# Jensen-Shannon divergence on one core: the bias of the logarithms as an immediate in place of a per-partition pointer

## The chip, the core and the metric

The kernel runs on one core of a Trainium2 chip. A core has several engines that run side by side, each with its own instruction queue: TensorE (PE, matmuls into PSUM), VectorE (DVE, elementwise work and reductions), ScalarE (ACT, functions from tables such as the logarithm), GpSimd (POOL) and SyncE (SP). SP, ACT and POOL can also start DMA transfers between the main memory (HBM) and the on-chip memory (SBUF). The metric is the time of one execution on the device in microseconds (us), the median of several; lower is better.

## What is computed

```python
def reference(p, q):                      # both 1024 x 4096, fp32, rows sum to 1
    m = 0.5 * (p + q)
    kl_pm = np.sum(p * np.log(p / (m + 1e-8) + 1e-8), axis=-1)
    kl_qm = np.sum(q * np.log(q / (m + 1e-8) + 1e-8), axis=-1)
    return (0.5 * (kl_pm + kl_qm)).astype(np.float32)      # 1024 values
```

The kernel takes the quotients apart: it forms ln(S·p), ln(S·q) and ln(S·(p+q)/2 + S·1e-8), with S = 6634 (`SHIFT`), stores the logarithms as 16-bit floats, and sums p·ln p + q·ln q − (p+q)·ln m over each row, times one half. The constant that is added inside a logarithm is the instruction's bias, the factor is its scale.

## The kernel before

The 1024 rows are cut into 8 row groups of 128 rows, one row to a partition, and each row group has 4096 columns. For every group there is one tile that holds p and q side by side as 16-bit floats. Three lists of widths, `LOADS`, `LOGS` and `SUMS`, cut the columns of every group into pieces: one for the transfers, one for the logarithms of p and q, one for the sum p+q and its logarithm. Pieces of different lists need not coincide. Row group 6, for instance, is loaded in two pieces of 2048 columns (loads 18 and 19), its logarithms are cut at 2304 (q18 and q19), and its sums at 1536 and 2816 (c21, c22, c23).

Loads. The first two pieces are loaded as fp32 by SP (p) and ACT (q), lines 153 and 154. All others are started by POOL (lines 161 and 162), which converts to 16 bits on the way. They are issued in the order of the columns, p and q in turn, and every load has a place of its own in SBUF, so no load waits for a buffer. At most eight of these transfers are under way: POOL waits for the landing of the one eight places before.

The operations, each with a letter and a number:
- F (line 203, PE): p+q of one sum piece, as matmuls with an identity matrix, into one of two PSUM buffers. For the first two pieces DVE adds instead (a, line 191).
- q (line 215, ACT): ln(S·p) and ln(S·q) of one log piece in a single instruction, into one of four buffers (tile `ab_t`). The bias is the tile `tiny_t`.
- c (line 223, ACT): ln of the sum of one sum piece, out of PSUM, into one of four buffers (tile `c_t`). The bias is the tile `epsc_t`.
- x (lines 234 and 238, DVE), row groups 0 to 2: the difference of the logarithms and its product with p and q.
- s (line 258, DVE), row groups 3 to 7: (p+q)·ln m with a running row sum, the sum read out by a small instruction right behind it.
- m (line 245, DVE), row groups 3 to 7: p·ln p and q·ln q. The last one, m24, is done with its row sum at line 251.
- r (line 272, PE): adds the columns of an x or m product into a PSUM accumulator, as matmuls with half the identity, in steps of 256 columns.
- f (lines 282 and 290, DVE): the final row sum of one row group out of the accumulator.

Every engine works through an order that is written out by hand (`ACT_ORDER`, `PE_ORDER`, `DVE_ORDER`, lines 58 to 72) and does not deviate from it. The last lines of ACT's order are `q18 c21 c22 q19 q20 c23 c24 q21 q22 c25 q23 c26 q24`, and of DVE's order `m18 s21 s22 m19 m20 s23 s24 m21 f6 m22 s25 m23 s26 f7 m24`. A c operation needs its F; an F from the fifth on needs its PSUM buffer back from the s (or c) two pieces before; an m needs its q, an s needs its c, f7 needs the matmuls on m23 and s26. At the end SP writes the result out (line 341).

Before all that, lines 147 to 150 write two one-column tiles with the biases on DVE, and line 156 runs one logarithm on a single column, so that ACT's table is loaded while the first data is on its way.

Of the kernel before, what the change touches and what calls it, by code (L numbers as in the profile page):

```python
# [9 lines left out]
SHIFT = 6634.0  # L10
# [65 lines left out]
def kernel(  # L76
# [6 lines left out]
    nc = tc.nc  # L83
    P = nc.NUM_PARTITIONS
    Alu = mybir.AluOpType
    Act = mybir.ActivationFunctionType
# [8 lines left out]
    fp32 = mybir.dt.float32  # L95
# [25 lines left out]
    small = ctx.enter_context(tc.tile_pool(name="small", bufs=1))  # L121
# [16 lines left out]
    def pq(g, c0, w):  # L138
        if g == 0:
            for i in range(HW):  # L140
                if loads[i] == (g, c0, w):
                    return early[i]
            c0 -= split
            assert c0 >= 0
        return data[g][:, :, c0 : c0 + w]

    tiny_t = small.tile([P, 1], fp32, tag="tiny")
    nc.vector.memset(tiny_t, 1e-30)  # L148
    epsc_t = small.tile([P, 1], fp32, tag="epsc")
    nc.vector.memset(epsc_t, SHIFT * 1e-8)  # L150
    for i in range(HW):
        g, c0, w = loads[i]
        nc.sync.dma_start(out=early[i][:, 0, :], in_=pv[g, :, c0 : c0 + w])
        nc.scalar.dma_start(out=early[i][:, 1, :], in_=qv[g, :, c0 : c0 + w])
    warm = small.tile([P, 1], fp32, tag="warm")
    nc.scalar.activation(out=warm, in_=tiny_t, func=Act.Ln, bias=tiny_t, scale=1.0)  # L156
    ident = small.tile([P, P], fp16, tag="ident")
    make_identity(nc, ident)
    for g, c0, w in loads[HW:]:
# [5 lines left out]
        out=half, in0=ident, scalar1=0.5, scalar2=0.0, op0=Alu.mult, op1=Alu.add  # L165
# [13 lines left out]
    ab, c, s, product, acc = {}, {}, {}, {}, {}  # L179
# [32 lines left out]
    def op_q(i):  # L212
        g, c0, w = logs[i]
        ab_t = lnp.tile([P, 2, w], fp16, tag="ab")
        nc.scalar.activation(  # L215
            out=ab_t, in_=pq(g, c0, w), func=Act.Ln, bias=tiny_t, scale=SHIFT
        )
        ab[i] = ab_t

    def op_c(j):  # L220
        w = parts[j][2]
        c_t = mid.tile([P, SW], fp16, tag="c")
        nc.scalar.activation(  # L223
            out=c_t[:, :w], in_=s[j], func=Act.Ln, bias=epsc_t, scale=SHIFT * 0.5
        )
        c[j] = c_t[:, :w]

# [73 lines left out]
    def uses(i):  # L301
# [16 lines left out]
        + [("s", j) for j in range(NS) if parts[j][0] == g and apart(parts[j])],  # L318
    }
    ops = dict(a=op_a, F=op_F, q=op_q, c=op_c, x=op_x, m=op_m, s=op_s, r=op_r, f=op_f)  # L320
    queues = [
        [(w[0], int(w[1:])) for w in text.split()] for text in (PE_ORDER, ACT_ORDER, DVE_ORDER)
# [49 lines left out]
```

## Time and profile before

| what | us |
|---|---|
| median of 9 runs | 103.49 (103.03 to 104.89) |
| the profiled execution, whole | 103.16 |
| its span, first to last instruction | 101.1 |
| ACT busy / DVE busy / PE busy | 92.7 / 82.1 / 64.2 |
| ACT waiting for loads (L215), three times in all | 2.0 |
| DVE waiting for ACT (L234 and L245) | 10.0 |
| last of the loads issued by POOL | 64.01 |
| last ACT logarithm begins | 95.92 |
| last DVE operation begins | 98.69 |

The span is what the profile shows; the whole time of an execution has another 2.06 us around it. A row of the profile gives engine, line, operation, output tile and input tiles, with shapes as partitions x elements. Tile names that are cut short, such as `t` for the data tiles and `st` for the sums in PSUM, are the program's own. A number in brackets behind a timeline row is how long the engine had been idle before it, and on what. DVE's 10.0 us is the sum of the rows of the view of the waits: 4.2 and 2.7 before line 234, 3.1 before line 245.

### The profile page before, as it was taken

The page shows a single profiled execution, that of the slowest core. Times are in us where ns is not written, and L with a number is a line of the kernel's source. Part 1 is how long each engine was busy: PE and PEld are TensorE (multiplying, and loading weights), DVE is VectorE, ACT ScalarE, POOL GpSimd, SP SyncE. Part 2 cuts the span into 40 slices and gives each one's busy share as a digit, 9 for nine tenths or more (in the row PEclk, how much of TensorE's full clock was granted, in tenths as well). Part 3 has the DMA queues.
Part 4 walks back from the last instruction along what each step waited for, and adds up shares of the span by engine and source line. Part 5 has one row for each costly group of instructions (what it writes and reads, how often), then busy time and mean ns, then how long its engine had stood idle before and what let it go on. Part 6 is the DMA issues. An engine that isn't in the chain of part 4 may idle for free.

```text
span 101.1 us, 1137 instructions
## 1 busy us (share of the span) xinstructions
PE 64.2 (64%) x402; PEld 39.6 (39%) x402; DVE 82.1 (81%) x88; ACT 92.7 (92%) x54; POOL 22.0 (22%) x46
## 2 busy tenths in 40 slices
PE   0048965576588674599669699248488197985250
PEld 0003534324255251445564474135173173834230
DVE  2179967688986935999999998399897999998980
ACT  3789999999999599999999999999999999999910
POOL 7955444242322422222222222200000000000000
PEclk9999999999999999759999999999999999999955
DMA  2999999999999999999999999999999940000000
GB/s 59 355 192 204 209 212 212 211 213 210 212 211 215 216 211 216 212 216 209 217 212 216 212 220 209 214 211 212 216 214 214 211 81 6 0 0 0 0 0 2
DMA packets 6485, 17.34 MB, mean 172 GB/s; under 512 B 848, under 2 KB 1872, under 8 KB 6480
## 3 DMA queue, kind: packets, MB, share of 16 engines
q0 software_dynamic: 5760, 16.29, 82.2%
q1 hardware_dynamic: 432, 0.50, 1.7%
q10 hardware_dynamic: 288, 0.49, 1.4%
q8 instruction: 3, 0.05, 0.2%
q14 instruction: 2, 0.02, 0.0%
HBM read 33.55 MB, written 0.00 MB: 332 GB/s over the span
## 4 chain that ended last, share of the span: by engine, by line
DMA 57%; ACT 18%; issue 11%; DVE 5%; POOL 4%; ACTq 1%; POOLq 0%; DVEq 0%
DMA t<-in_q_dram 57%; ACT ab_t L215 10%; ACT c_t L223 9%; DVE c_t L258 3%; POOL t L161 2%; POOL t L162 2%; ACTq L367 1%; DVE ab_t L245 1%; DVE ab_t L251 0%; DVE junk L290 0%; POOL ident masks.py:199 0%; POOL ident masks.py:197 0%; ACTq L215 0%; ACTq L223 0%; POOLq masks.py:199 0%
## 5 line engine op out<-in xcount | busy, mean ns | idle before, releaser
L215 ACT ACTIVATE ab_t<-t,tiny_t 128x2048 f16<-128x2048 f16 (+15 forms) x25 | 61.5, 2478 | 2.0 <-DMA t<-in_q_dram 2.0
L203 PE MATMUL st<-t,ident 128*128 128x512 f16 (+2 forms) x138 | 34.2, 376 | 13.8 <-DMA t<-in_p_dram 6.4
L272 PEld LDWEIGHTS <-half 128*128 128x128 f16 x264 | 26.1, 101 | 28.9 <-issue 23.7
L223 ACT ACTIVATE c_t<-st,epsc_t 128x1280 f16<-128x1280 f32 (+7 forms) x25 | 32.1, 1316 | 0.0
L272 PE MATMUL acc_t<-ab_t,half 128*128 128x256 f16 (+2 forms) x172 | 21.5, 279 | 14.0 <-DVE ab_t L245 13.7
L245 DVE TENSOR_TENSOR ab_t<-t,ab_t 128x2048 f16<-128x2048 f16 (+6 forms) x13 | 23.1, 1788 | 3.2 <-ACT ab_t L215 3.1
L203 PEld LDWEIGHTS <-ident 128*128 128x128 f16 x138 | 13.6, 101 | 28.6 <-issue 16.0
L234 DVE TENSOR_TENSOR ab_t<-ab_t,c_t 128x2048 f16<-128x2048 f16 (+8 forms) x12 | 14.7, 1224 | 6.9 <-ACT c_t L223 4.2
L258 DVE CUSTOM_DVE_ANT_0 c_t<-st,c_t,run 128x1280 f16<-128x1280 f32 (+3 forms) x10 | 16.0, 1602 | 0.7
L161 POOL DMA_DIRECT2D t<-in_p_dram x20 | 10.8, 541 | 22.3 <-DMA t<-in_p_dram 22.1
L272 PE MATMUL acc_t<-t,half 128*128 128x256 f16 (+1 forms) x92 | 11.8, 276 | 5.5 <-DVE t L238 5.5
L162 POOL DMA_DIRECT2D t<-in_q_dram x20 | 10.7, 535 | 19.7 <-DMA t<-in_q_dram 19.7
L238 DVE TENSOR_TENSOR t<-t,ab_t 128x2048 f16<-128x2048 f16 (+6 forms) x10 | 13.4, 1339 | 0.9
L258 DVE CUSTOM_DVE_ANT_0 c_t<-st,c_t 128x1536 f16<-128x1536 f32 (+1 forms) x5 | 8.2, 1645 | 0.0
L191 DVE TENSOR_TENSOR s<-t 128x320 f32<-128x320 f32 (+1 forms) x2 | 1.3, 658 | 3.2 <-DMA t<-in_q_dram 3.2
L156 ACT ACT_TABLE_LOAD x1 | 1.3, 1283 | 1.7 <-PEq L356 1.7
L290 DVE CUSTOM_DVE_ANT_0 junk<-acc_t,ones,run 128x256 f16<-128x256 f32 x5 | 2.4, 480 | 0.3
L238 DVE TENSOR_TENSOR ab_t<-t,ab_t 128x640 f16<-128x640 f32 (+1 forms) x2 | 2.3, 1158 | 0.1
L223 ACT ACTIVATE c_t<-s,epsc_t 128x320 f16<-128x320 f32 (+1 forms) x2 | 1.4, 679 | 0.0
L282 DVE TENSOR_REDUCE res<-acc_t 128x1 f32<-128x256 f32 x3 | 1.3, 418 | 0.0
L258 DVE DVE_READ_ACCUMULATOR2_ANT run<- 128x1 f32 x15 | 1.2, 83 | 0.0
L148 DVE MEMSET tiny_t<- 128x1 f32 x1 | 0.1, 59 | 0.8 <-PEq L356 0.8
(14 smaller groups left out, 2.7 us busy)
## 6 DMA issues: line engine op xcount, KB each, us to landing
t<-in_p_dram POOLq DMA_DIRECT2D x10, 512.0 KB, 19.4
t<-in_q_dram POOLq DMA_DIRECT2D x10, 512.0 KB, 19.4
t<-in_p_dram POOLq DMA_DIRECT2D x3, 320.0 KB, 13.4
t<-in_q_dram POOLq DMA_DIRECT2D x3, 320.0 KB, 13.3
t<-in_p_dram POOLq DMA_DIRECT2D x2, 352.0 KB, 10.8
t<-in_q_dram POOLq DMA_DIRECT2D x2, 352.0 KB, 11.5
t<-in_p_dram POOLq DMA_DIRECT2D x1, 384.0 KB, 12.8
t<-in_q_dram POOLq DMA_DIRECT2D x1, 384.0 KB, 13.3
```

The costliest lines, as they stand in the source:

```text
L156: nc.scalar.activation(out=warm, in_=tiny_t, func=Act.Ln, bias=tiny_t, scale=1.0)
L161: nc.gpsimd.dma_start(out=v[:, 0, :], in_=pv[g, :, c0 : c0 + w])
L162: nc.gpsimd.dma_start(out=v[:, 1, :], in_=qv[g, :, c0 : c0 + w])
L203: nc.tensor.matmul(out=st[:, b : b + m], lhsT=ident, rhs=v[:, t, b : b + m], start=t == 0, stop=t == 1,)
L215: nc.scalar.activation(out=ab_t, in_=pq(g, c0, w), func=Act.Ln, bias=tiny_t, scale=SHIFT)
L223: nc.scalar.activation(out=c_t[:, :w], in_=s[j], func=Act.Ln, bias=epsc_t, scale=SHIFT * 0.5)
L234: nc.vector.tensor_tensor(out=v, in0=v, in1=c[j].unsqueeze(1).to_broadcast([P, 2, w]), op=Alu.subtract)
L238: nc.vector.tensor_tensor(out=into, in0=u, in1=v, op=Alu.mult)
L245: nc.vector.tensor_tensor(out=ab[i], in0=u, in1=ab[i], op=Alu.mult)
L258: nc.vector.tensor_tensor_reduce(out=c[j], in0=s[j], in1=c[j], scale=-0.5, scalar=before, op0=Alu.mult, op1=Alu.add, accum_out=now,)
L272: nc.tensor.matmul(out=acc[g][:, :m], lhsT=half, rhs=v[:, t, b : b + m], start=k == terms_of[g][0] and n == 0, stop=k == terms_of[g][-1] a ...
L290: nc.vector.tensor_tensor_reduce(out=junk, in0=acc[g][:, :AW], in1=ones, scale=1.0, scalar=before, op0=Alu.mult, op1=Alu.add, accum_out=now,)
```

## The change

Both bias tiles and their memsets go. The logarithms at lines 215 and 223 take their bias as a number that stands in the instruction; scale, function, tiles and order stay. The warm-up logarithm takes a tile of its own, written by one memset, with the default bias and scale, in place of `tiny_t`. In the changed program the lines below the edit move up by three.

```diff
-    tiny_t = small.tile([P, 1], fp32, tag="tiny")
-    nc.vector.memset(tiny_t, 1e-30)
-    epsc_t = small.tile([P, 1], fp32, tag="epsc")
-    nc.vector.memset(epsc_t, SHIFT * 1e-8)
     for i in range(HW):
...
     warm = small.tile([P, 1], fp32, tag="warm")
-    nc.scalar.activation(out=warm, in_=tiny_t, func=Act.Ln, bias=tiny_t, scale=1.0)
+    nc.vector.memset(warm, 1.0)
+    nc.scalar.activation(out=warm, in_=warm, func=Act.Ln)
...
         nc.scalar.activation(
-            out=ab_t, in_=pq(g, c0, w), func=Act.Ln, bias=tiny_t, scale=SHIFT
+            out=ab_t, in_=pq(g, c0, w), func=Act.Ln, bias=1e-30, scale=SHIFT
         )
...
         nc.scalar.activation(
-            out=c_t[:, :w], in_=s[j], func=Act.Ln, bias=epsc_t, scale=SHIFT * 0.5
+            out=c_t[:, :w], in_=s[j], func=Act.Ln, bias=SHIFT * 1e-8, scale=SHIFT * 0.5
         )
```

## The prediction

> **What bounds the kernel now.** I read the page first (engine shares, the 40 slices, the costliest groups), then the waits, then ACT's and DVE's timelines, where the answer lies.
>
> From the page: the shares, two slice rows, and the two groups that the change edits.
>
> ```profile
> PE 64.2 (64%) x402; PEld 39.6 (39%) x402; DVE 82.1 (81%) x88; ACT 92.7 (92%) x54; POOL 22.0 (22%) x46
> ...
> ACT  3789999999999599999999999999999999999910
> ...
> DMA  2999999999999999999999999999999940000000
> ...
> L215 ACT ACTIVATE ab_t<-t,tiny_t 128x2048 f16<-128x2048 f16 (+15 forms) x25 | 61.5, 2478 | 2.0 <-DMA t<-in_q_dram 2.0
> ...
> L223 ACT ACTIVATE c_t<-st,epsc_t 128x1280 f16<-128x1280 f32 (+7 forms) x25 | 32.1, 1316 | 0.0
> ```
>
> ACT is at nine tenths in nearly every slice, so it looks like the bound. But the DMA row is as full until about slice 32 (83 us), and the loads write into tiles that nobody reuses, so their landings do not depend on compute. Two things pace the head: ACT, and a load stream that no ACT saving can hasten. ACT's timeline shows which one is last (start, duration, a merged pair counts as x2):
>
> ```profile
> 34.34 4.56 ACT L215 ACTIVATE ab_t<-t,tiny_t 128x5120 f16<-128x5120 f16 x1 [1.03 <-DMA t<-in_q_dram]
> ...
> 67.53 3.73 ACT L215 ACTIVATE ab_t<-t,tiny_t 128x4096 f16<-128x4096 f16 x1
> 71.12 2.57 ACT L223 ACTIVATE c_t<-st,epsc_t 128x1280 f16<-128x1280 f32 x2
> 73.67 4.13 ACT L215 ACTIVATE ab_t<-t,tiny_t 128x4608 f16<-128x4608 f16 x1
> 77.71 2.74 ACT L223 ACTIVATE c_t<-st,epsc_t 128x1536 f16<-128x1536 f32 x2
> ```
>
> The op at 73.67 is q18. Its 2304 columns of row group 6 reach into load 19, whose q half GpSimd issued at 54.18 (third from last on its timeline). Eight DMAs are in flight there and each takes 19.4 us to land (page, part 6), so it landed at about 73.57: q18 started some 0.1 us after its data, and was not more than that behind. The row at 34.34 is an earlier place of the same kind, with the wait visible.
>
> After 83 us no load is open. There the DVE timeline is the one to read (line 245 is an m op, 258 an s op, 290 an f op, 251 the last):
>
> ```profile
> 77.83 2.56 DVE L245 TENSOR_TENSOR ab_t<-t,ab_t 128x4608 f16<-128x4608 f16 x1 [0.44 <-ACT ab_t L215]
> ...
> 89.91 0.08 DVE L258 DVE_READ_ACCUMULATOR2_ANT run<- 128x1 f32 x1
> 90.08 1.23 DVE L245 TENSOR_TENSOR ab_t<-t,ab_t 128x2048 f16<-128x2048 f16 x1
> 91.22 0.48 DVE L290 CUSTOM_DVE_ANT_0 junk<-acc_t,ones,run 128x256 f16<-128x256 f32 x1
> 91.62 0.08 DVE L290 DVE_READ_ACCUMULATOR2_ANT res<- 128x1 f32 x1
> 91.97 1.23 DVE L245 TENSOR_TENSOR ab_t<-t,ab_t 128x2048 f16<-128x2048 f16 x1 [0.26 <-ACT ab_t L215]
> 93.29 1.68 DVE L258 CUSTOM_DVE_ANT_0 c_t<-st,c_t,run 128x1408 f16<-128x1408 f32 x1
> 94.90 0.08 DVE L258 DVE_READ_ACCUMULATOR2_ANT run<- 128x1 f32 x1
> 94.97 1.09 DVE L245 TENSOR_TENSOR ab_t<-t,ab_t 128x1792 f16<-128x1792 f16 x1
> 96.08 1.42 DVE L258 CUSTOM_DVE_ANT_0 c_t<-st,c_t,run 128x1152 f16<-128x1152 f32 x1
> 97.42 0.08 DVE L258 DVE_READ_ACCUMULATOR2_ANT run<- 128x1 f32 x1
> 97.65 0.48 DVE L290 CUSTOM_DVE_ANT_0 junk<-acc_t,ones,run 128x256 f16<-128x256 f32 x1
> 98.28 0.48 DVE L251 CUSTOM_DVE_ANT_0 ab_t<-t,ab_t,run 128x256 f16<-128x256 f16 x1
> ```
>
> DVE is almost without holes too: it idles at 77.4 for q18, then fractions of a tenth each time it meets a fresh ACT result. The end is set by two engines that run level, behind a load stream that sets their start.
>
> **What the Trainium skill says.** "ScalarE: Activation LUTs", section What ACT_TABLE_LOAD costs, prices an ACTIVATE with a `[128,1]` bias pointer at about 280 ns + 0.833 ns per element and one with immediates at 186 ns, 93 ns less; and says that neighbours overlap by about 93 ns. The trace agrees with the first: 2002 ns for the 2048 form (by-form groups; 280 + 1707 = 1987). The second price has no row here. "Perfetto Trace Analysis", section Optimizing Scalar/DVE Operations, gives the engine-busy overhead of ScalarE as about 93 ns on SBUF and 51 ns on PSUM, the rest of a profiled duration lying beside the next instruction. This lets me ask whether the pointer is in the part that blocks the engine. Start to start, the SBUF op of 3072 at 28.03 gives way to the next at 30.77: 2.74 − 2.56 = 0.18. The PSUM op of 1408 at 26.71 gives way at 28.03: 1.32 − 1.17 = 0.15. So 0.18 against 0.093, and 0.15 against 0.051: in both about 0.09 is over, which is the pointer's price. I take it that the pointer costs 93 ns of issue time. "TensorE: Matmul & The Clock Gate", Part 1, says that TensorE falls to half clock after an idle window of about 3.4 us; the page's PEclk row shows a 7 and a 5 once in mid-run, and 5s at the end.
>
> **The change, part by part.**
> *The 52 logarithms lose their pointer.* ACT's order is the same in the built program, and every wait names the same semaphores; each of L215's 25 and L223's 27 ops (a second row of the page has two of these) gets 93 ns shorter. Gross: 52 × 0.093 = 4.8 us. Bounds for one op: not below 0, as nothing is added to it, and not over the 0.15 to 0.18 of the whole fixed part; I take 0.093, and the end hangs little on it, as the tail below shows.
> *Ahead of q18* lie 39 of the 52, worth 3.6 us. All of it becomes waiting: q18 needs load 19 at 73.57 and started at 73.67, 0.1 later; the row at 34.34 shows ACT after a wait of this kind starting just behind its landing, too. Gain at q18's start: 0 (up to 0.1).
> *From q18 on* there are 13 ops (q18 c21 c22 q19 q20 c23 c24 q21 q22 c25 q23 c26 q24), back to back in the timeline. ACT alone ends 13 × 0.093 = 1.21 earlier. DVE can't take all of that. Its gaps against its own pace: m18 starts 0.09 earlier, as q18 ends 0.09 earlier. Then none to 89.91. From the accumulator read at 89.91 to m21 at 90.08: 0.17 (an m op can start with the read, as at 83.69). From the read at 91.62 to m22: 0.35. m22 to s25: 1.32, where the m op of the same width took 1.14 to its successor (90.08 to 91.22): 0.18. 94.90 to 94.97: 0.07. m23 to s26: 1.11 against 1.09 − 0.09 = 1.00 (a tensor_tensor's successor starts about 0.09 before its recorded end): 0.11. Sum 0.09 + 0.17 + 0.35 + 0.18 + 0.07 + 0.11 = 0.97. Each is within what ACT delivers by then: q21's end is 8 × 0.093 = 0.74 earlier where 0.26 is needed, q22's 0.84 (0.61), c25's 0.93 (0.79), q23's 1.02 (0.86), c26's 1.12 (0.97). So DVE, not ACT, sets the end, and does so for any price p from 0.08 up (12p at c26 against p + 0.88); at 0.18 the gain would be 1.06, at 0.05 it would be ACT's 0.6. What is late next is f7 (97.65): it also needs TensorE's matmuls on m23, 96.11 to 97.51. They follow m23, which comes 0.86 sooner, so end about 96.65; with some 0.05 of signalling f7 can start at 96.70, against 97.65 − 0.97 = 96.68 by DVE. That costs 0.02 to 0.03. Net: 0.94.
> *One memset less on DVE, and the warm-up's operands.* The two memsets took 0.06 each at 0.81; one stays, and ACT's table load to 2.94 covers it. The warm-up op gets 0.09 shorter before 3.24, under the first load, for which ACT idled 0.66: 0. No constant is added on GpSimd, whose list is the same, so no DMA issue moves.
> Sum: 103.16 (the profiled execution, 2.06 around its span of 101.1) − 0.94 = 102.22. That execution is 0.33 under the median 103.49 of the nine; on the median's level it is 102.55.
>
> **Rivals.**
> *A, the pointer's read hides in the overlap.* For it: the next op starts 93 ns ahead of its predecessor's recorded end (16.78 + 2.43 against 19.12), the same size as the price, so the price may be a latency. Against: the 0.18 and 0.15 above. Then only the ends come sooner, once and not per op: DVE gets 0.09 from q18 and up to that again at its tie points: 0.1, so 103.4.
> *B, the load stream is no wall.* Where the loads land earlier than in this profile, part of the 3.6 us counts, and with DVE's idle 0.44 ahead of m18: 0.97 + 0.44 = 1.4 to 1.6, so 101.9. Against: the DMA row has no slack, and its landings don't hang on ACT.
> *C, slower: TensorE at half clock in the tail.* With ACT waiting for loads, TensorE's idle gaps (up to 3.4 us, before its L272 matmuls) may fall in another phase. Place: the 14 + 8 matmuls for m19 and m20 and the six of F25, 85.76 to 89.72. c25, due at 91.0 after the change, has 1.3 us to spare, so 2.5 us of half clock costs nothing. From 4.4 us on (two stretches such as the one in mid-run), the 0.94 is gone; with the whole stretch at half clock, F25 ends near 93.1, s25 starts at 94.5 in place of 93.29: +1.2, so 104.7.
> That the change doesn't do what it says is small: the built list has no bias operand left.
>
> **How the numbers follow.** Forecast 0.66 (its own range 102.2 to 102.9, from ±0.3 of the executions and 0.05 per step), A 0.14, B 0.09, C 0.08, and 0.03 for a drift of the chip to either side. Predicted 102.6. Range 101.9 to 103.4: it takes in B's and A's ends, and leaves out C and half of the drift. A measurement of this kernel tells 0.5% (0.52 us) from no change. Faster: nearly all of the forecast and B, 0.74. Same: A and a little of the forecast, 0.16. Slower: C and drift, 0.10.
>
> **What would show it.** L215's 2048 form at about 1910 ns and L223's 1280 form at about 1235; q18 still near 73.7, with waits on DMA ahead of it adding up to over 3 us on ACT; from there DVE without gaps, its last op about 0.95 earlier. Wrong if the starts of ACT's ops keep their distances though the durations fall (A), if q18 moves (B), or if PEclk shows half clock between 85 and 93 (C).

## The result, and the profile after

The changed kernel takes 102.50 us in the median (101.99 to 103.56, 18 runs) against 103.73 us before (102.90 to 105.04, 55 runs). The ratio is 0.9892, with a 95% interval of 0.9873 to 0.991: faster by 1.1%, or 1.1 us. The medians are over all runs, while this ratio and those below leave out runs of over 1.5% above the fastest of their kernel, so a ratio and the quotient of two medians need not agree.

These are rows of the page of the changed kernel: the shares, the ACT and clock slices, and the two groups of logarithms (lines 212 and 220, which were 215 and 223 before):

```profile
PE 67.9 (67%) x402; PEld 41.8 (41%) x402; DVE 81.7 (81%) x87; ACT 89.0 (88%) x54; POOL 21.9 (22%) x46
...
ACT  3689998999999499999998999997969999999910
...
PEclk9999999999999999556999999985999957999995
...
L212 ACT ACTIVATE ab_t<-t 128x2048 f16<-128x2048 f16 (+15 forms) x25 | 59.4, 2388 | 4.6 <-DMA t<-in_q_dram 4.3
...
L220 ACT ACTIVATE c_t<-st 128x1280 f16<-128x1280 f32 (+7 forms) x25 | 30.0, 1222 | 1.0 <-PE st L200 0.9
```

The mean of the q ops fell from 2478 to 2388 ns and that of the c ops from 1316 to 1222: 90 and 94 ns each. ACT is 3.7 us less busy. Its waits inside these two groups grew from 2.0 to 5.6 us at the same time (4.6 + 1.0), so the greater part of what ACT saved has turned into waiting, mostly for loads.

ACT's timeline of the changed kernel shows where (start, duration, idle time before and its releaser):

```profile
34.18 4.47 ACT L212 ACTIVATE ab_t<-t 128x5120 f16<-128x5120 f16 x1 [1.44 <-DMA t<-in_q_dram]
...
56.18 2.35 ACT L220 ACTIVATE c_t<-st 128x1280 f16<-128x1280 f32 x2
58.41 5.42 ACT L212 ACTIVATE ab_t<-t 128x2048 f16<-128x2048 f16 x2
...
70.70 2.53 ACT L220 ACTIVATE c_t<-st 128x1280 f16<-128x1280 f32 x2 [0.68 <-PE st L200]
74.21 4.04 ACT L212 ACTIVATE ab_t<-t 128x4608 f16<-128x4608 f16 x1 [0.98 <-DMA t<-in_q_dram]
...
85.81 2.75 ACT L220 ACTIVATE c_t<-st 128x1280 f16<-128x1280 f32 x2 [0.21 <-PE st L200]
```

The same place in the profile before:

```profile
56.77 2.54 ACT L223 ACTIVATE c_t<-st,epsc_t 128x1280 f16<-128x1280 f32 x2
59.19 5.61 ACT L215 ACTIVATE ab_t<-t,tiny_t 128x2048 f16<-128x2048 f16 x2
```

Two c ops of 1280 start at 56.18 and are followed at 58.41: 1.12 us for each. Before, such a pair ran from 56.77 to 59.19, 1.21 each. The starts have come together by 0.09 and not only the ends. q18, at 74.21, stands idle 0.98 us for load 19, where it had stood at 73.67 with next to no wait.

This one execution took 103.12 us (span 101.1) and so lies above the median of its kernel. Two things in it differ from the profile before: q18 got its data 0.54 later, and TensorE's clock was at half for about 3.4 us from 67.6 and again from 81.2 (the 5s of the PEclk row), so that c19 and c23 waited for their sums. Neither belongs to the edit as far as the profiles show: in three profiles of runs below with the same short logarithms in the head, q18 starts at 73.42 to 73.67, and a kernel with all its pointers (the warm-up alone, below) has the half clock at the same two places. Measured from q18's start the execution is faster: from there to the last DVE op (line 248, 98.64 for its read-out) are 24.43 us, before 98.69 − 73.67 = 25.02. That is 0.59 of the gain; the rest has to be looked for in an execution without these two differences, and the experiments give one.

### The profile page after: what moved, and what is told of

Same layout as the page of the kernel before. It is cut to its first block, busy times and chain, and to the rows that moved or that the text cites. A ratio compares the mean times of both kernels' runs of the same rounds, so it can differ in the third digit from the quotient of the medians.

```text
span 101.1 us, 1136 instructions
## 1 busy us (share of the span) xinstructions
PE 67.9 (67%) x402; PEld 41.8 (41%) x402; DVE 81.7 (81%) x87; ACT 89.0 (88%) x54; POOL 21.9 (22%) x46
## 4 chain that ended last, share of the span: by engine, by line
DMA 69%; ACT 10%; PE 6%; DVE 5%; issue 3%; POOL 2%; ACTq 1%; POOLq 0%; DVEq 0%
DMA t<-in_q_dram 69%; ACT ab_t L212 9%; PE acc_t L269 4%; DVE ab_t L242 3%; PE st L200 2%; DVE c_t L255 1%; ACTq L364 1%; POOL t L158 1%; ACT c_t L220 1%; POOL t L159 1%; DVE ab_t L248 0%; DVE junk L287 0%; POOL ident masks.py:199 0%; POOL ident masks.py:197 0%; ACTq L212 0%
## 5 line engine op out<-in xcount | busy, mean ns | idle before, releaser
L212 ACT ACTIVATE ab_t<-t 128x2048 f16<-128x2048 f16 (+15 forms) x25 | 59.4, 2388 | 4.6 <-DMA t<-in_q_dram 4.3
L200 PE MATMUL st<-t,ident 128*128 128x512 f16 (+2 forms) x138 | 36.0, 395 | 13.9 <-DMA t<-in_p_dram 7.1
L269 PEld LDWEIGHTS <-half 128*128 128x128 f16 x264 | 27.6, 106 | 25.8 <-issue 18.6
L220 ACT ACTIVATE c_t<-st 128x1280 f16<-128x1280 f32 (+7 forms) x25 | 30.0, 1222 | 1.0 <-PE st L200 0.9
L269 PE MATMUL acc_t<-ab_t,half 128*128 128x256 f16 (+2 forms) x172 | 23.1, 292 | 11.4 <-DVE ab_t L242 11.4
L200 PEld LDWEIGHTS <-ident 128*128 128x128 f16 x138 | 14.3, 106 | 29.2 <-issue 16.7
L269 PE MATMUL acc_t<-t,half 128*128 128x256 f16 (+1 forms) x92 | 13.2, 298 | 3.9 <-DVE t L235 3.9
L220 ACT ACTIVATE c_t<-s 128x320 f16<-128x320 f32 (+1 forms) x2 | 1.2, 586 | 0.0
```

The lines of the kernel that those rows point to most:

```text
L200: nc.tensor.matmul(out=st[:, b : b + m], lhsT=ident, rhs=v[:, t, b : b + m], start=t == 0, stop=t == 1,)
L212: nc.scalar.activation(out=ab_t, in_=pq(g, c0, w), func=Act.Ln, bias=1e-30, scale=SHIFT)
L220: nc.scalar.activation(out=c_t[:, :w], in_=s[j], func=Act.Ln, bias=SHIFT * 1e-8, scale=SHIFT * 0.5)
L269: nc.tensor.matmul(out=acc[g][:, :m], lhsT=half, rhs=v[:, t, b : b + m], start=k == terms_of[g][0] and n == 0, stop=k == terms_of[g][-1] a ...
```

## The experiments

The question was where in the row of 52 shorter logarithms the gain comes from, and what limits it. The main theory is that of the prediction: the load stream sets q18's start, ops behind it count, and DVE limits what they bring.

**Only the 13 logarithms from q18 on, and only the 39 ahead of it.**

```diff
-  func=Act.Ln, bias=tiny_t, scale=SHIFT
+  func=Act.Ln, bias=1e-30 if i >= 18 else tiny_t, scale=SHIFT          # first run
+  func=Act.Ln, bias=1e-30 if i < 18 else tiny_t, scale=SHIFT           # second run
...
-  func=Act.Ln, bias=epsc_t, scale=SHIFT * 0.5
+  func=Act.Ln, bias=SHIFT * 1e-8 if j >= 21 else epsc_t, scale=SHIFT * 0.5   # first run
+  func=Act.Ln, bias=SHIFT * 1e-8 if j < 21 else epsc_t, scale=SHIFT * 0.5    # second run
```

> Immediate bias only in the 13 logarithms from q18 on, pointers in the 39 before it. Theory (the load stream sets q18's start, so only the ops behind it count): nearly the whole gain of the change, 0.9 to 1.2 us under the kernel before, q18 near 73.7. Rival (every op counts alike): a quarter of it, about 0.3 us.

> Immediate bias only in the 39 logarithms ahead of q18, pointers from q18 on. Theory: 0 to 0.2 us under the kernel before, with over 2 us more of ACT's time in waits for loads. Rival (every op counts alike): about 0.8 us under it.

Measured: the tail alone 0.9924 (0.9897 to 0.9951), or 0.8 us, a little under the 0.9 to 1.2 that were expected; the head alone 0.9986 (0.9962 to 1.001), or 0.1 us. A quarter of the ops brings most of the gain and three quarters bring nothing that can be told from zero. In the profile of the run with the head alone, most of the time that ACT saved has become waits. This is the view of ACT's waits there:

```profile
ACT ab_t L215 <- DMA t<-in_q_dram: 3.6, 7, 1.6
...
ACT c_t L223 <- PE st L203: 0.9, 1, 0.9
ACT ab_t L215 <- ACT ab_t L215: 0.3, 1, 0.3
```

Together 4.8 us, against 2.0 before: 2.8 more, of the 3.6 that 39 ops save. Nine waits in place of three also end six of the overlaps of 0.09 between neighbours, by estimate another 0.5. q18 starts at 73.63, against 73.67 before.

**The warm-up alone.** The kernel before with the new warm-up, everything else with pointers:

```diff
-    nc.scalar.activation(out=warm, in_=tiny_t, func=Act.Ln, bias=tiny_t, scale=1.0)
+    nc.vector.memset(warm, 1.0)
+    nc.scalar.activation(out=warm, in_=warm, func=Act.Ln)
```

> The kernel before with the new warm-up alone (own tile, one memset more, default bias); all other logarithms keep their pointers. Theory: 0, within 0.2 us, as ACT waits 0.66 us for the first load behind it. Rival (the start of the kernel counts): 0.1 us or more either way in every run.

Measured: 0.9999 (0.9978 to 1.002). No change that can be told from zero, as expected.

**One pointer more.** The scale becomes a pointer as well, so that each logarithm has two:

```diff
+    sc_t = small.tile([P, 1], fp32, tag="sc")        # memset to SHIFT; sch_t the same with SHIFT * 0.5
-  func=Act.Ln, bias=tiny_t, scale=SHIFT
+  func=Act.Ln, bias=tiny_t, scale=sc_t
-  func=Act.Ln, bias=epsc_t, scale=SHIFT * 0.5
+  func=Act.Ln, bias=epsc_t, scale=sch_t
```

> The kernel before with the scale of every logarithm as a second per-partition pointer, so one pointer more in place of one less. Theory (93 ns of issue time for each pointer, the load stream hides a faster ACT but not a slower one): starts of a 1280 form 1303 ns apart; ACT loses its 1.0 us of waiting ahead of the 5120 form, the other 2.6 us of the head and 1.1 us of the tail count: 3.4 to 3.8 us slower than before. Rival A (the read hides in the overlap): durations 93 ns longer, starts as before, 0.1 us slower. Rival (gain and loss of the same size): 1.1 us slower.

Measured: 1.0327 (1.0283 to 1.037), or 3.4 us slower, at the lower edge of what the theory gave. ACT's timeline in this run, at the place shown above and at q18:

```profile
57.99 2.75 ACT L227 ACTIVATE c_t<-st,epsc_t,sch_t 128x1280 f16<-128x1280 f32 x2
60.59 5.82 ACT L219 ACTIVATE ab_t<-t,tiny_t,sc_t 128x2048 f16<-128x2048 f16 x2
...
76.11 4.22 ACT L219 ACTIVATE ab_t<-t,tiny_t,sc_t 128x4608 f16<-128x4608 f16 x1
```

A pair of 1280 ops takes 2.60, or 1.30 each, against 1.21 with one pointer and 1.12 with none: each pointer costs the engine 0.09. The price is the same in both directions, while the effect on the time is three times as large when ACT gets slower. q18 starts 2.44 later than before, with no wait ahead of it: a slower ACT is not hidden by the loads, a faster one is. Rival A, a price in latency alone, is out.

**Taking q18 off the load that it waits for.** The logarithms of row group 6 are cut at 2048 in place of 2304, so that q18 needs load 18 alone. The same cut is made in the changed kernel and in the one before:

```diff
 LOGS = [
...
-    [2304, 1792],
+    [2048, 2048],
```

> The changed kernel with the logarithms of row group 6 cut at 2048 in place of 2304, so that q18 needs load 18 alone and not load 19. Theory: ACT no longer waits about 1 us ahead of q18, which starts near 73.2, and DVE's 2.1 us of idle time ahead of m18 shrinks; 1.0 to 1.3 us under the changed kernel, some 2.2 under the kernel before. Rival (DVE's work alone sets the end, whenever q18 starts): as the changed kernel, 1.1 under before.

> The kernel before with the same cut at 2048. Theory: with pointers ACT reaches q18 at about the time that load 19 lands, so moving the dependence to load 18 gives little, 0 to 0.4 us. Rival (the load stream was the wall by itself, in the kernel before as well): about 1 us, as in the changed kernel.

Measured: with immediates 0.9813 (0.9757 to 0.9869), 1.9 us under before and 0.8 under the changed kernel by the two ratios; with pointers 0.9966 (0.9938 to 0.9995), 0.35 us. That the cut is worth more where ACT is ahead of the loads agrees with load 19 holding the changed kernel back, but with intervals as wide as these, 0.8 can't be told from 0.35; a clearer pair follows below. Nor is it settled whether the first is short of its 1.0 to 1.3, as its interval takes in the 2.2 us under before that were expected. Its ACT timeline shows one wait that the theory had left out:

```profile
71.47 2.37 ACT L220 ACTIVATE c_t<-st 128x1280 f16<-128x1280 f32 x2 [0.61 <-PE st L200]
73.72 3.62 ACT L212 ACTIVATE ab_t<-t 128x4096 f16<-128x4096 f16 x1
```

q18 no longer waits for a load, but c19 waits 0.61 us for its sum from TensorE, whose clock was at half there again. So TensorE's clock was the next suspect, and it got experiments of its own.

**Keeping TensorE busy.** 44 matmuls of zeros (the w operations) are put into TensorE's waits for DVE. They go into the accumulators of the row groups that are next, and change no sum:

```diff
+FILL = [(5, 16), (5, 8), (6, 12), (7, 8)]        # row group, number
 PE_ORDER = """
...
-F15 F16 r14 r15 F17 F18 r16 r17 F19 F20 r18 F21 F22 r19 F23 F24 r20 r21 F25 F26 r22 r23
-r24
+F15 F16 r14 r15 F17 F18 r16 w0 r17 F19 F20 w1 r18 F21 F22 w2 r19 F23 F24 r20 r21 F25 F26 r22 r23
+w3 r24
...
+    def op_w(i):
+        g, count = FILL[i]
...
+        for n in range(count):
+            nc.tensor.matmul(
+                out=acc[g][:, :AW], lhsT=half, rhs=zeros, start=g not in started, stop=False
+            )
```

> The changed kernel with 44 matmuls of zeros put into TensorE's waits ahead of the products m16, m17, m18 and m23 (they add nothing to the sums), so that it isn't idle there. Theory: the half clock between 67.5 and 71 and between 81 and 84.5 goes away, and with it ACT's 0.9 us of waits for F; 0.2 to 0.5 us under the changed kernel, 1.3 to 1.6 under before. Rival (TensorE's clock costs the end nothing): as the changed kernel, or slower by what the added matmuls delay.

> The kernel before with the same added matmuls, as a control. Theory: ACT has no slack there that the clock could take, and the profile of before shows full clock at these places, 0 to 0.3 us under before. Rival (the clock costs the kernel before as much as the changed one): 0.3 to 0.5 us under before.

> The changed kernel with the added matmuls of zeros, 28 in place of 12 ahead of m18's. Theory: the half clock that was left near 80 to 84 us goes away, and c23 no longer waits for F23; the tail is then as the sum of the prediction has it, 0.9 to 1.0 us under the kernel before with the added matmuls, 1.5 to 1.7 under before. Rival (what is left of the clock costs the end nothing): as with 12, 1.3 under before; or slower, where the added matmuls hold up m18's.

Measured: the changed kernel with 44 of them 0.9875 (0.9847 to 0.9903), with 60 of them (28 in place of the 12) 0.9875 (0.9851 to 0.9899), the kernel before 0.994 (0.9906 to 0.9975). Against the changed kernel's 0.9892 that is 0.2 us, within the intervals. The profile with 44 still has one stretch of half clock, from 80.3 us; in the profile with 60 it is gone, and the time is the same, under the 1.5 to 1.7 us that were expected. So this stretch cost nothing that can be told from zero: there the rival was right. The control came out above its 0 to 0.3: the kernel before gains 0.6 us by the ratio (0.3 to 1.0). How much of that the matmuls bring is open, because two of the thirteen runs without them that are compared took 104.71 and 104.75 us and the other eleven 103.23 to 104.02; the median of those eleven lies 0.5 above the 103.19 with the matmuls.

The profile with 60 is the execution that was wanted: its q18 starts at 73.67, to the hundredth where it did before, though now after a wait of 1.33 us for the load, and the clock is full from 45 us up to the last slice. Its DVE timeline is to be set beside the one in the prediction (lines 246, 259, 303 and 252 are now m, s, f and the last):

```profile
77.75 2.56 DVE L246 TENSOR_TENSOR ab_t<-t,ab_t 128x4608 f16<-128x4608 f16 x1 [1.52 <-ACT ab_t L216]
...
89.82 0.09 DVE L259 DVE_READ_ACCUMULATOR2_ANT run<- 128x1 f32 x1
89.82 1.22 DVE L246 TENSOR_TENSOR ab_t<-t,ab_t 128x2048 f16<-128x2048 f16 x1
90.96 0.48 DVE L303 CUSTOM_DVE_ANT_0 junk<-acc_t,ones,run 128x256 f16<-128x256 f32 x1
91.36 0.08 DVE L303 DVE_READ_ACCUMULATOR2_ANT res<- 128x1 f32 x1
91.36 1.22 DVE L246 TENSOR_TENSOR ab_t<-t,ab_t 128x2048 f16<-128x2048 f16 x1
92.50 1.68 DVE L259 CUSTOM_DVE_ANT_0 c_t<-st,c_t,run 128x1408 f16<-128x1408 f32 x1
94.10 0.08 DVE L259 DVE_READ_ACCUMULATOR2_ANT run<- 128x1 f32 x1
94.10 1.09 DVE L246 TENSOR_TENSOR ab_t<-t,ab_t 128x1792 f16<-128x1792 f16 x1
95.11 1.41 DVE L259 CUSTOM_DVE_ANT_0 c_t<-st,c_t,run 128x1152 f16<-128x1152 f32 x1
96.44 0.09 DVE L259 DVE_READ_ACCUMULATOR2_ANT run<- 128x1 f32 x1
96.67 0.48 DVE L303 CUSTOM_DVE_ANT_0 junk<-acc_t,ones,run 128x256 f16<-128x256 f32 x1
```

Every gap that the prediction's sum counted is closed: the m op at 89.82 starts with the read ahead of it, and so do those at 91.36 and 94.10. What is left is 0.14 ahead of f7, where the profile before has 0.15. f7 starts at 96.67, where the sum had put it at 96.70, 0.98 earlier than before.

**A version faster than both.** The first run has the cut at 2048 together with the 44 matmuls. The second has two more cuts of the same kind: row group 2's logarithms at 2560 as well, so that q10 needs load 10 alone, and row group 3's at 2048. This makes one q operation more, so that in the second run the numbers from q11 on move up by one in the three orders.

```diff
 LOGS = [
...
-    [1536, 2560],                  # second run only
-    [1792, 2304],                  # second run only
+    [1536, 1024, 1536],
+    [2048, 2048],
...
-    [2304, 1792],                  # both runs
+    [2048, 2048],
```

> The changed kernel with row group 6 cut at 2048 and with the same added matmuls. Theory: without the half clock ahead of c19 and c20, q18 starts near 73.2 instead of 73.7; 0.3 to 0.6 us under the run with the cut alone, 2.2 to 2.5 under before. Rival: as the cut alone, 1.9 under before.

> The run with the even cut and the added matmuls, and in addition the logarithms of row group 2 cut at 2560 (q10 needs load 10 alone) and those of row group 3 cut at 2048. Theory: ACT's wait of 1.8 us near 34 us shrinks to what load 12 or 13 leave, some 0.5 to 1.0 us under the run without these two cuts, 3.2 to 3.7 under before. Rival (DVE, which shows no wait after 66 us there, sets the end by its own work): 0 to 0.2 us.

Measured: 0.9739 (0.9713 to 0.9764), 100.89 us in the median; and 0.9716 (0.968 to 0.9752), 100.57 us. The first, 2.7 us under before, gained a little more than the theory had. Against 0.9875 with the 44 matmuls alone, the cut is worth 1.4 us here, and these two intervals lie well apart: load 19 does hold back the kernel with immediates. (The kernel before was not run with both the cut and the matmuls.) ACT's timeline, with the earlier wait for a load:

```profile
34.70 4.47 ACT L216 ACTIVATE ab_t<-t 128x5120 f16<-128x5120 f16 x1 [1.82 <-DMA t<-in_q_dram]
...
54.68 2.12 ACT L216 ACTIVATE ab_t<-t 128x2304 f16<-128x2304 f16 x1 [0.27 <-ACT ab_t L216]
...
70.41 2.38 ACT L224 ACTIVATE c_t<-st 128x1280 f16<-128x1280 f32 x2
72.65 3.65 ACT L216 ACTIVATE ab_t<-t 128x4096 f16<-128x4096 f16 x1
```

ACT reaches q18 at 72.65 without any wait. The second falls short of 3.2 to 3.7 us with 2.9, and the intervals of the two overlap. Its ACT timeline shows where its gain went:

```profile
43.98 3.62 ACT L216 ACTIVATE ab_t<-t 128x4096 f16<-128x4096 f16 x1 [0.18 <-DMA t<-in_q_dram]
...
54.11 2.12 ACT L216 ACTIVATE ab_t<-t 128x2304 f16<-128x2304 f16 x1 [0.73 <-DMA t<-in_q_dram]
...
72.09 3.65 ACT L216 ACTIVATE ab_t<-t 128x4096 f16<-128x4096 f16 x1
```

The wait of 1.82 us at 34.70 is gone, but the op at 54.11, which reaches into load 15, now waits 0.73 where it waited 0.27, and q18 (q19 in this run), at 72.09, starts only 0.56 earlier. Whether the times differ by it is not settled.

## Why the prediction was right

- *The price of a pointer is issue time.* Right: 90 and 94 ns by the means of the two groups (1906 and 1228 ns for the forms at 2048 and 1280, where 1910 and 1235 were forecast), and the distance of the starts falls by 0.09 per op and rises by 0.09 with a second pointer. This agrees with the price of about 93 ns in the Trainium skill's "ScalarE: Activation LUTs", section What ACT_TABLE_LOAD costs, and settles what its sentence on overlapping neighbours left open in this case: the pointer is not in the overlapped part.
- *The head is absorbed at q18.* Right. The head alone gives 0.1 us. Not all of it became waiting for loads: 0.9 us of ACT's waits in the head's own run are for TensorE's sums, which the prediction had not counted there. One reading was off without effect: the issue at 54.18 is the fifth from last on GpSimd's timeline, and the third from last only among those for q.
- *The tail's sum.* Right in its mechanism: 0.94 against a measured 1.1 (0.9 to 1.3 by the interval). In the execution with q18 at the same time as before, f7 comes 0.98 earlier where 0.95 was forecast, and DVE has no gap left but the 0.14 ahead of f7, so it, and not ACT, sets the end there. The 0.02 to 0.03 for TensorE's matmuls on m23 did not come up: they took 1.40 us before, for the greater part at half clock, and 0.93 at full clock in this execution, where they ended at 96.17. That 102.6 fell so close to 102.50 is in part luck: the kernel before was set at 103.49 from nine runs and measured 103.73 over 55, and the gain came out above 0.94.
- *The warm-up and the memset at nothing.* Right, 0.9999.
- *Rival B.* The load stream is a wall. In the four profiles with immediates in the whole head and the old cut (the changed kernel, the head alone, 44 and 60 matmuls), q18 starts at 74.21, 73.63, 73.42 and 73.67, each time after a wait for its load, against 73.67 before.
- *Rival C.* The half clock did come, but ahead of the place named: from 81.2 to 84.6 us, on the matmuls for m18 and on F23, and once more in the head. In the place named, 85.76 to 89.72, the clock was full. Where c23 waited 0.21 us for it, the time without it was no different. That such stretches never cost anything is not shown: of the 19 executions of the changed kernel, the five with a mean clock of 0.919 to 0.921 took 102.74 to 103.12 us and the four with 0.960 to 0.962 took 101.99 to 102.40.
- *What stays open.* Whether the measured 1.1 is more than the 0.94 because the kernel before loses more by TensorE's clock: with the 44 matmuls added to both, the two ratios give 0.9875 / 0.994 = 0.9935, or 0.7 us, and the medians of the two, 102.40 and 103.19, lie 0.8 apart, but the intervals are too wide to tell this from 0.94 or from 1.1. The profiles of the kernel before with and without these matmuls both show full clock from 46 us up to the last slices, so no profile shows what the matmuls save there.

## What to carry to other kernels

Ask of an engine that is 92% busy what it will wait for once it is faster: here three quarters of the saving ran into a load that, by the prediction's estimate, landed 0.1 us ahead of its use, and nearly all of the gain came from what lay behind that load. A fixed saving per instruction is worth most where no stream takes it up as waiting. Once it has been made, the cuts of the work should be moved to the landings: the same cut was worth about 0.35 us before the change, about 0.8 us after it, and 1.4 us with TensorE kept busy (the first two with intervals that overlap). A bias that is one number for all partitions belongs in the instruction, which saved 0.09 us for each logarithm here.

## What was not expected of the hardware

TensorE is 64% busy and looked irrelevant, yet the executions of the changed kernel with less of the full clock took longer, as said under rival C. What brings the half clock was not as expected either. The Trainium skill's "TensorE: Matmul & The Clock Gate", Part 1, gives one idle window of about 3.4 us as what sends TensorE to half clock, and says that this window is free-running. In the profile of the changed kernel the half clock came twice in the second half, each time for about 3.4 us, near waits of 3.0 and 4.1 us for DVE. These are the clock rows of three more pages: of the kernel before, of the run with the warm-up alone, and of the changed kernel with 44 matmuls of zeros:

```profile
PEclk9999999999999999759999999999999999999955
...
PEclk9999999999999999999999999966999859999975
...
PEclk9999999999999999999999999999999958999999
```

In the first, a wait of 3.41 us ahead of 67.2 us was followed by full clock; in the second, also a kernel with all its pointers, the clock fell to half at 66.7, within a wait of the same 3.41 us that ended at 67.0. That fits a window that runs free of the program, and suggests that the half clock at this place is a matter of chance from one execution to the next. The third does not fit an idle window of 3.4 us: there the clock fell to half at 80.3 us after a wait of only 2.06 us, ahead of 80.1, with zeros and other matmuls until 78.0. A wait shorter than the window was enough, and the gap of 3.0 us in the changed kernel was, too. Which share of a window must be idle is not shown here.
